# A fp32 encoder block on one core: weight tiles in pairs, and two tiles of a product in one VectorE instruction

## The chip, the cores and the metric

The kernel runs on one core of a Trainium2 chip. The metric is device time in microseconds (us), the median of the runs. A core has TensorE (PE, matmuls), VectorE (DVE), ScalarE (ACT), GpSimd (POOL) and SyncE (SP), each with a queue that it works off in order. They meet through semaphores. Here SP issues nearly all transfers, and POOL some that add to what lies in memory.

## The reference, cut to what matters

One layer over x of 256 rows and 1024 columns, all in fp32. The weight matrices make up nearly all of the traffic and of the matmuls:

```python
x = x + 0.5 * rmsnorm(swiglu(rmsnorm(x), w_in, w_down))        # FFN 1, d_ff 2816
h = rmsnorm(x); z = h @ w_in                                   # one wide projection
A = hgrn2(q, f, i, g)                                          # gated linear recurrence, chunks of 64
B = fox_attention(q, k, v, f)                                  # causal attention with forget gates
y = sigmoid(gate_A) * (A @ w_branch_a) + sigmoid(gate_B) * (B @ w_branch_b)
x = x + rmsnorm(y @ w_out)
x = x + rmsnorm(cross_attention(rmsnorm(x), rmsnorm(mem)))     # 4 heads, memory of 256 rows
x = x + 0.5 * rmsnorm(swiglu(rmsnorm(x), w_in, w_down))        # FFN 2
```

## The kernel before, in words

**Split operands.** Each fp32 operand is kept as a high part `hi` (a cast to fp32r on ACT) and a low part `lo` (source minus high part, a subtraction on DVE). A product is three matmuls: high by high, low by high, high by low (`MM`, L100). Activations and weights are both split, and the split of the weights is most of the work of DVE and ACT.

**Units.** The weights come as units of 128 x 1024 fp32 (512 KB). `load_split` loads one into a tile `raw` (SP), casts it (ACT, L153) and makes the low part (DVE, L155). `unit` does so on first use and keeps the tiles. Four memory tags matter: `raw` and `extra` with four tiles each, `hi` and `lo` with eight each. A tile is used again, in turn, once every reader of its last contents is done. `extra` also serves things that are not weights: some of the first loads (`head`), the recurrence's scratch (`early`, `qf`), the split keys `kp`, `brow`, `pT1`, `memT`, and the sums `ss`.

**Pairs of seven products.** In eight places (columns c = 4, 6, 9 of the first FFN and 3, 6, 9 of the second, one branch projection and the memory's value projection) two adjacent column blocks are computed by a scheme of seven products in place of eight. It needs sums of weight blocks. `sum_load` or `pair_load` fetches two tiles `sraw` from `extra`; POOL adds further blocks by transfers that accumulate (`more`, `pair_more`). `raws` fetches two plain blocks. `add` adds blocks on DVE, tile by tile (L596 in the FFNs, L1393 in the other two); `splits` casts and splits the two tiles one after the other (`split`, L173 and L174). Between the products PE does other work, in the FFNs mostly the down projection (`acc`).

**What sets the order.** A scheduler orders each engine's instructions by its own estimates and by priorities, under the constraints written in the code; each engine then runs its list in order. A change in the size of an instruction therefore changes the lists of all engines.

Of the kernel before, what the change touches and what calls it, by code (L numbers as in the profile page):

```python
# [18 lines left out]
P = 128  # L19
D = 1024  # L20
# [65 lines left out]
def block_kernel(ctx: ExitStack, tc: tile.TileContext, wts, head_in, gf_in, x_in, mem_in, memT_in, cols, rows, fbias, masks, out):  # L86
# [57 lines left out]
    def load_split(src, n=512, behind=None, parts=None):  # L144

        raw = wp.tile([P, D], F32, tag="raw", name=nm("raw"), bufs=4)
        hi, lo = parts or parts_of()
        r, h, l = raw, hi, lo
        if n < 512:
            r, h, l = (p.rearrange("p (k n) -> p k n", k=2)[:, :, :n] for p in (raw, hi, lo))  # L150
        loads.append(nc.sync.dma_start(r, src).ins)
        with tc.issue_after(behind[0]) if behind else nullcontext():
            casts.append(S.copy(h, r).ins)  # L153
        with tc.issue_after(behind[1]) if behind else nullcontext():
            los.append(V.tensor_tensor(out=l, in0=r, in1=h.bitcast(F32), op=ALU.subtract).ins)  # L155
        return hi, lo

    def unit(name, i):
        u = _AT[name] + i
        if u not in cache:  # L160
            cache[u] = load_split(wts[u - 4], behind=hold.get(u), parts=place.get(u))
        return cache[u]

    def chunk(name, c):
# [7 lines left out]
    def split(hi, lo, src):  # L172
        a = S.copy(hi, src)  # L173
        b = V.tensor_tensor(out=lo, in0=src, in1=hi.bitcast(F32), op=ALU.subtract)  # L174
        return a.ins, b.ins

    class Pair:

# [248 lines left out]
    def ffn(w_in, w_dn, X, r2, n_tok, i_row, first_half, second_half=None):  # L427
# [126 lines left out]
            return out, q, parts  # L554

        def sum_load(c, n, halves):
            t = []
            for j in range(2):
                r = wp.tile([P, D], F32, tag="extra", name=nm("sraw"), bufs=4)
                more(r, c, *halves[0], j, None)  # L560
                t.append(r)
            return t

        def more(r, c, k, n, j, op):
# [6 lines left out]
        def act_pair(c, between):  # L571
# [5 lines left out]
            def of_x(k):  # L577
                return lambda kk: (X.hi(4 * k + kk, 0, P), X.lo(4 * k + kk, 0, P))

            def splits(t):  # L580
                u = []
                for r in t:
                    p = parts_of()
                    split(p[0], p[1], r)
                    u.append(p)
                return u

            def raws(k, n):
                t = [wp.tile([P, D], F32, tag="raw", name=nm("raw"), bufs=4) for _ in range(2)]
                for j in range(2):  # L590
                    more(t[j], c, k, n, j, None)
                return t

            def add(t, o):
                for x, y in zip(t, o):
                    V.tensor_tensor(out=x, in0=x, in1=y, op=ALU.add)  # L596

            def product(ps, stat, u, start):
                for kk in range(4):
# [20 lines left out]
            add(sums, both)  # L620
            if c in FETCHED[w_in]:
                for j in range(2):
                    more(both[j], c, 1, 1, j, ALU.add)
            for _ in range(2 if c == 3 else 1):
                step_between()
            b4 = mm()
# [169 lines left out]

    X1 = Joined()
    xf1 = [m4([P, 4, T], n="xf") for _ in range(2)]  # L800
    heads, raw1 = [], []
    for kb in range(KB):
        heads.append(wp.tile([P, D], F32, tag="extra" if kb in (1, 2, 3, 4, 6) else "raw", name=nm("head"), bufs=4))
        n = HX if kb == 0 else 0
        if n:
            nc.scalar.dma_start(heads[kb][:, :n], head_in[kb, :, :n])
        loads.append(nc.sync.dma_start(heads[kb][:, n : HX + 512], head_in[kb, :, n:]).ins)
        if kb % 2 == 0:
            raw1.append(wp.tile([P, D], F32, tag="extra" if kb == 6 else "raw", name=nm("raw"), bufs=4))
# [10 lines left out]
    for kb in range(KB):  # L820
        if kb % 2 == 0:
            for c in range(2):
                cache[_AT["f1_in"] + 4 * c + kb // 2] = parts_of()
        for c in range(2):
            hi, lo = (p[:, kb % 2 * 512 : kb % 2 * 512 + 512] for p in cache[_AT["f1_in"] + 4 * c + kb // 2])
            w = heads[kb][:, HX : HX + 512] if c == 0 else raw1[kb // 2][:, kb % 2 * 512 : kb % 2 * 512 + 512]
            with tc.issue_after(lo_last):
                S.copy(hi, w)
# [29 lines left out]
    for i in range(2):  # L858
        place[_AT["i_a"] + i] = [wp.tile([P, D], F32R, tag="extra", name=nm("w"), bufs=4) for _ in range(2)]
    iv = [m4([P, 2, 512], n="iv") for _ in range(2)]  # L860
    for h in range(2):
        m = len(log)
# [77 lines left out]
    class Rec:  # L940


        def __init__(self, g):
            self.g, self.f = g, fT[g]
            self.aux = m4([P, D], n="aux")

            self.ATd = self.aux[:, 256:512]

            self.Es = wp.tile([P, D], F32, tag="extra", name=nm("early"), bufs=4)
            self.K, self.Q0 = kT_[g], qT_[g]  # L950
            self.Q = wp.tile([P, D], F32, tag="extra", name=nm("qf"), bufs=4).rearrange("p (b h t) -> p b h t", b=2, h=4)
# [131 lines left out]
    zf = [s1(8, name="zf") for _ in range(2)]  # L1083
    gf_last = {}
    for c in range(3):
        u = [load_split(gf_in[4 * c + i], GF) for i in range(4)]
        n = min(GF, D - c * GF)
        for h in range(2):
            ps = mm()
# [88 lines left out]

    kq = []
    for g in range(2):  # L1180
        kp = [wp.tile([P, D], F32R, tag="extra", name=nm("kp"), bufs=4).rearrange("p (i t) -> p i t", i=4) for _ in range(2)]
# [75 lines left out]

    def fox_pT(g, m):
        pT0 = m4([P, 4, T], n="pT0")
        pT1 = wp.tile([P, D], F32, tag="extra", name=nm("pT1"), bufs=4)[:, :512].rearrange("p (i s) -> p i s", i=4)  # L1260
        for h, b in ((0, 0), (1, 0), (1, 1)):
            tr = trp()
            with after(m + 5 * b):
# [43 lines left out]
    def gates(c):  # L1307
        u = chunk("gates", c)
        z = m4([P, 2, 512], n="zg")
        if c < 2:  # L1310
            brow = wp.tile([P, D], F32, tag="extra", name=nm("brow"), bufs=4)[:, :512]
# [57 lines left out]
        return wts[_AT[name] + 4 * (1 - n) + 2 * k + j - 4]  # L1369

    def pair_load(name, k, n, tag):
        t = []
        for j in range(2):
            r = wp.tile([P, D], F32, tag=tag, name=nm("sraw" if tag == "extra" else "raw"), bufs=4)
            loads.append(nc.sync.dma_start(r, pair_block(name, k, n, j)).ins)
            t.append(r)
        return t

    def pair_more(name, t, k, n):
        for j in range(2):  # L1380
            G.dma_start(t[j], pair_block(name, k, n, j), accum_op=ALU.add)

    def splits(t):
        u = []
        for r in t:
            p = parts_of()
            split(p[0], p[1], r)
            u.append(p)
        return u

    def add(t, o):
        for x, y in zip(t, o):
            V.tensor_tensor(out=x, in0=x, in1=y, op=ALU.add)  # L1393

    def product(ps, stat, u, start):
        for kk in range(4):
# [97 lines left out]
    next(pair)  # L1494
    summed(1, 1)

    memT_s = [wp.tile([P, 4, T], F32, tag="extra", name=nm("memT"), bufs=4) for _ in range(2)]
    for j in range(2):
        nc.sync.dma_start(memT_s[j], memT_in[:, 4 * j : 4 * j + 4, :])
    M = Joined()  # L1500
# [50 lines left out]
                half(X3, r3, c, G_MEM, m + (L_WO, L_MK)[c], m + (L_WO, L_MK)[c] + 16)  # L1551
    def mem_sums():
        a, b, d, e = (memT_s[k][:, :, h * P : h * P + P] for h in range(2) for k in range(2))
        ss = [wp.tile([P, 2, 4, P], F32, tag="extra", name=nm("ss"), bufs=4) for _ in range(2)]
# [140 lines left out]
    g3 = load_row(2)  # L1695
    for kb in range(4):
        hold[_AT["mo"] + kb] = marks[(1, 1, 3, 3)[kb]]
    for i in range(2):
        place[_AT["f2_in"] + i] = [wp.tile([P, D], F32R, tag="extra", name=nm("w"), bufs=4) for _ in range(2)]
    X4 = Joined()  # L1700
    r4 = [None, None]
    po = [[acc(), acc()], [acc(), acc()]]
# [110 lines left out]
```

## Time and profile before

| | |
|---|---|
| median of 3 runs | 767.61 us (767.55 to 768.75) |
| the profiled execution, first to last instruction | 765.6 us, mean granted clock 0.997 |
| around it, by the median | 2.0 us |
| PE busy | 756.7 us (99%) |
| DVE busy | 670.7 us (88%), 988 instructions |
| ACT busy | 520.6 us (68%), 841 instructions |
| read from memory | 152.91 MB, 201 GB/s over the span |

The page names lines and tiles: `lo<-sraw,hi` at L174 is a low part in a pair, `lo<-raw,hi` at L155 that of a unit. `DVE lo L155 <- ACT hi L153` says that DVE stood still until ACT had made that high part. In timelines the columns are start, duration, engine and line, with the idle time before it and its cause in brackets. x2 means two instructions in a row, whose time is given together.

### The profile page before, as it was taken

How to read it: one execution, taken by the hardware profiler on the slowest of the kernel's cores; microseconds unless marked ns; L12 is line 12 of the kernel's file. 1: busy time of each engine (PE TensorE's matmuls, PEld its weight loads, DVE VectorE, ACT ScalarE, POOL GpSimd, SP SyncE). 2: the span in 40 equal slices, each digit the busy share in tenths (PEclk: the TensorE clock that was granted, in tenths of full speed). 3: DMA queues.
4: the chain of work that ended last, by engine and by line, in shares of the span. 5: the costliest groups of instructions: out<-in, count | busy, mean ns of one | idle time of the engine just before them, and what ended most of it. 6: DMA issues, size and time to landing. Idle time of an engine off the chain costs nothing.

```text
span 765.6 us, 11740 instructions
## 1 busy us (share of the span) xinstructions
PE 756.7 (99%) x4302; PEld 642.1 (84%) x4302; DVE 670.7 (88%) x988; ACT 520.6 (68%) x841; POOL 27.2 (4%) x50
## 2 busy tenths in 40 slices
PE   9999999999999999999999999999999999999996
PEld 7888888888888998898888888888888888888885
DVE  6799998998678898888689888999989999998983
ACT  7677576688774669667567754875868567675662
POOL 0000000000000100200000000001000000000000
PEclk9999999999999999999999999999999999999998
DMA  9768677674655535835668965476386716558341
GB/s 344 238 257 247 212 240 275 170 261 174 223 169 149 185 122 185 290 135 163 210 220 226 267 202 184 160 284 130 124 283 202 251 66 232 208 191 288 125 140 55
DMA packets 46282, 154.73 MB, mean 202 GB/s; under 512 B 5289, under 2 KB 9009, under 8 KB 46225
## 3 DMA queue, kind: packets, MB, share of 16 engines
q1 hardware_dynamic: 43168, 144.83, 55.0%
q0 software_dynamic: 2624, 8.80, 6.4%
q8 instruction: 33, 0.54, 0.3%
q10 hardware_dynamic: 432, 0.37, 0.2%
q14 instruction: 25, 0.20, 0.1%
HBM read 152.91 MB, written 1.06 MB: 201 GB/s over the span
## 4 chain that ended last, share of the span: by engine, by line
PE 83%; DVE 9%; DMA 3%; ACT 2%; issue 2%; SPq 0%; POOL 0%; DVEq 0%; ACTq 0%; POOLq 0%
PE mm L100 44%; PE acc L100 30%; PE tr L100 5%; DVE lo L155 2%; DMA raw<-in_wts_dram 1%; PE tr L445 1%; DVE lo L174 1%; ACT hi L153 1%; DMA head<-in_head_dram 1%; DMA row<-rd 1%; PE tr L385 1%; DVE sraw L1393 1%; DVE xs L421 0%; DVE memT L1505 0%; DVE sx L174 0%
## 5 line engine op out<-in xcount | busy, mean ns | idle before, releaser
L155 DVE TENSOR_TENSOR lo<-raw,hi 128x1024 fp32r<-128x1024 f32 (+1 forms) x188 | 222.3, 1199 | 28.2 <-ACT hi L153 25.0
L153 ACT CAST hi<-raw 128x1024 fp32r<-128x1024 f32 (+1 forms) x188 | 190.5, 1032 | 48.5 <-DMA raw<-in_wts_dram 26.0
L100 PE MATMUL mm<-hi,hlT 128*128 128x512 f32 (+1 forms) x632 | 191.4, 381 | 0.0
L100 PEld LDWEIGHTS mm<-hi,hlT 128*128 128x128 f32 x632 | 116.8, 188 | 20.2
L100 PE MATMUL mm<-lo,hlT 128*128 128x512 f32 (+1 forms) x316 | 119.1, 381 | 0.0
L100 PE MATMUL acc<-hi,act 128*128 128x512 f32 x352 | 113.6, 390 | 0.0
L173 ACT CAST hi<-sraw 128x1024 fp32r<-128x1024 f32 x80 | 83.3, 1052 | 35.5 <-DVE sraw L596 17.5
L174 DVE TENSOR_TENSOR lo<-sraw,hi 128x1024 fp32r<-128x1024 f32 x80 | 96.0, 1220 | 1.7 <-ACT hi L173 1.4
L100 PE MATMUL mm<-hi,sx 128*128 128x512 f32 x280 | 90.7, 391 | 0.0
L100 PEld LDWEIGHTS acc<-hi,act 128*128 128x128 f32 x352 | 66.1, 188 | 13.4
L100 PE MATMUL acc<-lo,act 128*128 128x512 f32 x176 | 69.5, 395 | 0.0
L100 PEld LDWEIGHTS mm<-lo,hlT 128*128 128x128 f32 x316 | 59.3, 188 | 10.0
L100 PEld LDWEIGHTS mm<-hi,sx 128*128 128x128 f32 x280 | 52.5, 188 | 10.9
L100 PE MATMUL acc<-hlT,hi 128*128 128x512 f32 x240 | 60.9, 394 | 0.2 <-DVE hlT L373 0.2
L100 PE MATMUL mm<-lo,sx 128*128 128x512 f32 x140 | 54.9, 392 | 0.0
L100 PEld LDWEIGHTS acc<-hlT,hi 128*128 128x128 f32 x240 | 43.1, 189 | 8.2 <-DVE hlT L373 0.7
L174 DVE TENSOR_TENSOR lo<-raw,hi 128x1024 fp32r<-128x1024 f32 x32 | 38.3, 1220 | 2.4 <-ACT hi L173 2.3
L173 ACT CAST hi<-raw 128x1024 fp32r<-128x1024 f32 x32 | 33.0, 1052 | 9.1 <-DMA raw<-in_wts_dram 3.9
L100 PEld LDWEIGHTS acc<-lo,act 128*128 128x128 f32 x176 | 33.1, 188 | 6.4
L100 PE MATMUL acc<-lo,hT 128*128 128x512 f32 x96 | 37.8, 393 | 0.0
L100 PE MATMUL acc<-hi,hT 128*128 128x512 f32 x96 | 37.6, 392 | 0.1
L100 PE MATMUL acc<-hi,lT 128*128 128x512 f32 x96 | 37.3, 390 | 0.0
(329 smaller groups left out, 1232.1 us busy)
## 6 DMA issues: line engine op xcount, KB each, us to landing
raw<-in_wts_dram SPq DMA_DIRECT2D x215, 512.0 KB, 4.5
sraw<-in_wts_dram SPq DMA_DIRECT2D x32, 512.0 KB, 5.8
sraw<-in_wts_dram POOLq DMA_DIRECT2D x14, 512.0 KB, 5.9
raw<-in_gf_dram SPq DMA_DIRECT2D x12, 344.0 KB, 3.5
head<-in_head_dram SPq DMA_DIRECT2D x7, 392.0 KB, 6.4
grow<-in_rows_dram SPq DMA_DIRECT2D x4, 512.0 KB, 7.6
xs<-in_x_dram SPq DMA_DIRECT2D x2, 512.0 KB, 7.7
cb<-cd POOLq DMA_DIRECT2D x2, 512.0 KB, 5.3
```

What stands on the lines that cost most here:

```text
L100: log.append(PE.matmul(*args, **kw).ins)
L153: casts.append(S.copy(h, r).ins)
L155: los.append(V.tensor_tensor(out=l, in0=r, in1=h.bitcast(F32), op=ALU.subtract).ins)
L173: a = S.copy(hi, src)
L174: b = V.tensor_tensor(out=lo, in0=src, in1=hi.bitcast(F32), op=ALU.subtract)
L385: PE.transpose(blocks[-1][1], src(kb), ident)
L445: PE.transpose(trv[:, j, h * P : (h + 1) * P], ats[c, h][:, j * P : (j + 1) * P], ident)
L1393: V.tensor_tensor(out=x, in0=x, in1=y, op=ALU.add)
```

## The change: what it does

Every buffer of the four tags is a pair of tiles side by side, `[128, 2, 1024]`, with half as many of them, so that the memory is the same. A pair's tile is one object: it is used again when both halves are done. Within the pairs of seven products DVE makes the low parts of both halves by one subtraction of 128 x 2048 (L205), and adds both by one addition (L209). The casts stay one for each half (L204). Units are loaded two at a time; their casts (L177) and low parts (L172) stay one for each. What else used `extra` gets halves of a pair in turn (`extra`), and the first loads likewise halves of `raw` (`raw_half`).

```diff
+    def double(tag, name=None, dt=F32):
+        return wp.tile([P, 2, D], dt, tag=tag, name=nm(name or tag), bufs=4 if tag in ("hi", "lo") else 2)
+
     def parts_of():
-        return [wp.tile([P, D], F32R, tag=t, name=nm(t), bufs=8) for t in ("hi", "lo")]
...
+        return [double(t, dt=F32R) for t in ("hi", "lo")]
...
+    def extra(name, dt=F32):
+
+        if "extra" not in spare:
+            t = double("extra", name, F32)
+            spare["extra"] = t[:, 1]
+            r = t[:, 0]
+        else:
+            r = spare.pop("extra")
+        return r if dt is F32 else r.bitcast(dt)
...
+        for j in range(2):
+            loads.append(nc.sync.dma_start(r[:, j], srcs[j]).ins)
+            with tc.issue_after(behind[j][0]) if behind[j] else nullcontext():
+                casts.append(S.copy(h[:, j], r[:, j]).ins)
+            low(j, behind[j])
...
+    def splits(t):
+        p = parts_of()
+        for j in range(2):
+            S.copy(p[0][:, j], t[:, j])
+        V.tensor_tensor(out=p[1], in0=t, in1=p[0].bitcast(F32), op=ALU.subtract)
+        return halves_of(p)
+
+    def add(t, o):
+        V.tensor_tensor(out=t, in0=t, in1=o, op=ALU.add)
...
-            def splits(t):
-                u = []
-                for r in t:
-                    p = parts_of()
-                    split(p[0], p[1], r)
-                    u.append(p)
-                return u
...
-            def add(t, o):
-                for x, y in zip(t, o):
-                    V.tensor_tensor(out=x, in0=x, in1=y, op=ALU.add)
...
-            self.Es = wp.tile([P, D], F32, tag="extra", name=nm("early"), bufs=4)
+            self.Es = extra("early")
```

The first place is column 6 of the first FFN. On DVE before, from the adds of the two sums to the low parts of the third product (`sraw_944` and `sraw_946` are the sum's two tiles, `act` an activation's low part, `raw_1074` and `raw_1086` units of the down projection):

```order
L596 TENSOR_TENSOR sraw_944<-sraw_944,raw_1047 128x1024
L596 TENSOR_TENSOR sraw_946<-sraw_946,raw_1048 128x1024
L174 TENSOR_TENSOR act_628<-tr_978,act_628 128x512
L174 TENSOR_TENSOR lo_1054<-sraw_944,hi_1053 128x1024
L174 TENSOR_TENSOR lo_1058<-sraw_946,hi_1057 128x1024
L155 TENSOR_TENSOR lo_1076<-raw_1074,hi_1075 128x1024
L155 TENSOR_TENSOR lo_1088<-raw_1086,hi_1087 128x1024
```

On DVE now, from the add of the second product on (`lo_940` belongs to it, `lo_974` to the third, `lo_993` to the pair of units):

```order
L209 TENSOR_TENSOR sraw_878<-sraw_878,sraw_881 128x2048
L198 TENSOR_TENSOR act_597<-tr_907,act_597 128x512
L205 TENSOR_TENSOR lo_940<-sraw_878,hi_939 128x2048
L209 TENSOR_TENSOR sraw_878<-sraw_878,raw_969 128x2048
L205 TENSOR_TENSOR lo_974<-sraw_878,hi_973 128x2048
L172 TENSOR_TENSOR lo_993<-raw_991,hi_992 128x1024 x2
```

The add and the low part that needs it are now neighbours, and the act's low part has come ahead of `lo_940`. On ACT before, at the same place:

```order
L173 CAST hi_1014<-sraw_944 128x1024
L173 CAST hi_1018<-sraw_946 128x1024
L617 COPY vw_954<-mm_956 128x512
L173 CAST act_628<-tr_978 128x512
L173 CAST hi_1053<-sraw_944 128x1024
L173 CAST hi_1057<-sraw_946 128x1024
L153 CAST hi_1075<-raw_1074 128x1024
L153 CAST hi_1087<-raw_1086 128x1024
L173 CAST hi_1098<-raw_1047 128x1024
L630 COPY pc_955<-mm_1013 128x512
```

On ACT now (`vw` and `pc` are copies of a finished product out of PE's accumulators):

```order
L204 CAST hi_939<-sraw_878 128x1024
L637 COPY vw_886<-mm_888 128x512
L197 CAST act_597<-tr_907 128x512
L204 CAST hi_939<-sraw_878 128x1024
L204 CAST hi_973<-sraw_878 128x1024
L650 COPY pc_887<-mm_938 128x512
L204 CAST hi_973<-sraw_878 128x1024
L177 CAST hi_992<-raw_991 128x1024 x2
```

The second cast of `hi_939` stands behind a copy and a cast that wait for PE, and the second of `hi_973` behind the copy of the product before it.

The second place is the end of the memory's value projection, under the softmax. On ACT before (`pm` are the exponentials, `hi_5816` and `hi_5820` the sixth product's two tiles):

```order
L173 CAST hi_5816<-raw_5812 128x1024
L173 CAST hi_5820<-raw_5814 128x1024
L1649 ACT_TABLE_LOAD
L1649 ACTIVATE pm_5726,sm_5720<-acc_5693,mx_5719,sc_5691 128x256 x2
...
L298 ACT_TABLE_LOAD
L298 ACTIVATE warm_79<-ones 128x1
L173 CAST hT_5780<-cv_5782 128x512
L173 CAST hi_5836<-sraw_5580 128x1024
```

On ACT now (`hi_5449` is the sixth product's pair):

```order
L204 CAST hi_5449<-raw_5446 128x1024
L1664 ACT_TABLE_LOAD
...
L332 ACT_TABLE_LOAD
L332 ACTIVATE warm_79<-ones 128x1
L197 CAST hT_5417<-cv_5419 128x512
L1629 COPY pc_5241<-mm_5242 128x512
L204 CAST hi_5449<-raw_5446 128x1024
```

The second half's cast has moved from ahead of the eight exponentials to behind them.

The third place is column 3 of the second FFN, on DVE (`sx` are low parts of activation sums). Before:

```order
L596 TENSOR_TENSOR sraw_6528<-sraw_6528,raw_6653 128x1024
L174 TENSOR_TENSOR act_6410<-tr_6600,act_6410 128x512
L174 TENSOR_TENSOR sx_6525<-ss_6514,sx_6525 128x512
L596 TENSOR_TENSOR sraw_6530<-sraw_6530,raw_6654 128x1024
L174 TENSOR_TENSOR lo_6660<-sraw_6528,hi_6659 128x1024
L174 TENSOR_TENSOR lo_6664<-sraw_6530,hi_6663 128x1024
```

Now:

```order
L198 TENSOR_TENSOR act_6013<-tr_6188,act_6013 128x512
L198 TENSOR_TENSOR sx_6122<-ss_6111,sx_6122 128x512
L209 TENSOR_TENSOR sraw_6125<-sraw_6125,raw_6235 128x2048
L209 TENSOR_TENSOR sraw_6128<-sraw_6128,raw_6235 128x2048
L198 TENSOR_TENSOR sx_6244<-ss_6111,sx_6244 128x512
L205 TENSOR_TENSOR lo_6240<-sraw_6125,hi_6239 128x2048
```

The add now starts behind act and sx, and a second one, which had come earlier before, stands between it and the low part.

More of the change, by code (lines that the diff above doesn't have):

```diff
@@ L622, in act_pair @@
                 for j in range(2):
-                    more(both[j], c, 1, 1, j, ALU.add)
+                    more(both[:, j], c, 1, 1, j, ALU.add)
             for _ in range(2 if c == 3 else 1):
@@ L802, in block_kernel @@
     for kb in range(KB):
-        heads.append(wp.tile([P, D], F32, tag="extra" if kb in (1, 2, 3, 4, 6) else "raw", name=nm("head"), bufs=4))
+        heads.append(extra("head") if kb in (1, 2, 3, 4, 6) else raw_half("head"))
         n = HX if kb == 0 else 0
@@ L1371, in pair_load @@
     def pair_load(name, k, n, tag):
[L1372 removed]
+        t = double(tag, "sraw" if tag == "extra" else "raw")
         for j in range(2):
[L1374 to L1376 removed]
+            loads.append(nc.sync.dma_start(t[:, j], pair_block(name, k, n, j)).ins)
         return t
@@ L1380, in pair_more @@
         for j in range(2):
[L1381 to L1393, printed above, removed]
+            G.dma_start(t[:, j], pair_block(name, k, n, j), accum_op=ALU.add)
     def product(ps, stat, u, start):
@@ L1495, in block_kernel @@
     summed(1, 1)
-    memT_s = [wp.tile([P, 4, T], F32, tag="extra", name=nm("memT"), bufs=4) for _ in range(2)]
+    memT_s = [extra("memT").rearrange("p (k t) -> p k t", k=4) for _ in range(2)]
     for j in range(2):
@@ L1697, in block_kernel @@
         hold[_AT["mo"] + kb] = marks[(1, 1, 3, 3)[kb]]
-    for i in range(2):
-        place[_AT["f2_in"] + i] = [wp.tile([P, D], F32R, tag="extra", name=nm("w"), bufs=4) for _ in range(2)]
+    place[_AT["f2_in"]] = [double("extra", "w", F32R) for _ in range(2)]
     X4 = Joined()
```

63 lines of the change are left out of this document (35 added, 28 removed).

## The prediction

> **What bounds the kernel now.** I first read the page's busy times and the chain that ended last.
>
> ```profile
> PE 756.7 (99%) x4302; PEld 642.1 (84%) x4302; DVE 670.7 (88%) x988; ACT 520.6 (68%) x841; POOL 27.2 (4%) x50
> PE 83%; DVE 9%; DMA 3%; ACT 2%; issue 2%; SPq 0%; POOL 0%; DVEq 0%; ACTq 0%; POOLq 0%
> ```
>
> TensorE is busy for 756.7 of 765.6 us and carries 83% of the chain. A busy PE need not be PE at its peak, so next I asked what PE waited for (total us, times, longest), and how full the engines are in one early stretch (PE, PEld, DVE, ACT, POOL).
>
> ```profile
> PE tr L100 <- PEq L1802: 0.8, 1, 0.8
> PE acc L100 <- ACT hlT L372: 0.5, 1, 0.5
> PE acc L1662 <- DVE sm L1652: 0.3, 1, 0.3
> PE acc L100 <- ACT hi L828: 0.3, 1, 0.3
> PE acc L100 <- DVE hlT L373: 0.2, 1, 0.2
> 75.00:100.00 25.00, 25.00 (x116) 20.69 (x115) 24.92 (x28) 15.51 (x21) 1.69 (x2) 1.00 0.77 222
> ```
>
> These are all of PE's waits: 2.1 us. The granted clock is 1.00. So no more than 2.1 us can be won while the matmuls stay the same in number and size, which they do. But between 75 and 100 us VectorE is as full as PE, 24.92 of 25 us: what delays VectorE there soon delays PE. The kernel has little to win and much to lose.
>
> **The change, part by part: VectorE's own work.** The instructions that are merged, one by one, and a half-sized one for the slope:
>
> ```profile
> L174 DVE TENSOR_TENSOR lo<-sraw,hi 128x1024 fp32r<-128x1024 f32 x80 | 96.0, 1220 | 1.7 <-ACT hi L173 1.4
> L596 DVE TENSOR_TENSOR sraw<-sraw,raw 128x1024 f32<-128x1024 f32 x30 | 36.1, 1219 | 0.0
> L174 DVE TENSOR_TENSOR act<-tr,act 128x512 fp32r<-128x512 f32 x22 | 15.1, 686 | 1.7 <-ACT act L173 1.6
> ```
>
> 112 low parts become 56 and 50 adds become 25: 81 fewer. From 512 to 1024 columns the time grows by 1220 - 686 = 534 ns, so 2048 columns should take 1220 + 2 x 534 = 2288 ns. The trace has no such instruction. Its upper bound is two single ones, 2.44 us; I take the slope, 2.29. By durations a merge saves 0.15 us, but two back to back take 2.35 us together in the timeline below, so in a full queue it saves 0.06. Over 81 merges that is 5 to 12 us of VectorE time. PE waited for VectorE 0.5 us in all, so none of this is on PE's path by itself. The lower bound on its worth is zero.
>
> The Trainium skill ("Perfetto Trace Analysis", section "Optimizing Scalar/DVE Operations") puts a fixed cost of about 60 ns on each VectorE operation in SBUF and says that larger operations raise throughput where the engine is saturated. The back-to-back rows agree with the 60 ns. The same section says that where an engine is not saturated but makes bubbles on others, breaking instructions up lets work finish sooner. By the first rule the full window above should gain; by the second the change should lose. The rows below decide it.
>
> **What the merge does to the order of events.** The chain in a product is add, cast on ScalarE, low part. It overlapped tile by tile: the first tile was cast while the second was added. After the change no cast can start before the whole add has ended, and no low part before both casts have. The place to see it is the second pair of the first FFN (the ACT and DVE rows of the order are in the section on the change). Before, on DVE and then ACT:
>
> ```profile
> 96.94 2.36 DVE L596 TENSOR_TENSOR sraw<-sraw,raw 128x1024 f32<-128x1024 f32 x2
> 99.21 0.69 DVE L174 TENSOR_TENSOR act<-tr,act 128x512 fp32r<-128x512 f32 x1
> 99.81 2.35 DVE L174 TENSOR_TENSOR lo<-sraw,hi 128x1024 fp32r<-128x1024 f32 x2
> ...
> 96.18 0.59 ACT L617 COPY vw<-mm 128x512 f32<-128x512 f32 x1 [2.96 <-PE mm L100]
> 96.66 0.59 ACT L173 CAST act<-tr 128x512 fp32r<-128x512 f32 x1
> 98.19 2.18 ACT L173 CAST hi<-sraw 128x1024 fp32r<-128x1024 f32 x2 [0.94 <-DVE sraw L596]
> 104.43 0.58 ACT L630 COPY pc<-mm 128x512 f32<-128x512 f32 x1
> ```
>
> And what PE had there:
>
> ```profile
> 98.71 0.39 PE L100 MATMUL mm<-hi,sx 128*128 128x512 f32 x1
> ...
> 104.15 0.39 PE L100 MATMUL mm<-hi,sx 128*128 128x512 f32 x1
> ```
>
> The isolated chain now takes 2.29 + 2.1 (two casts) + 2.29 = 6.7 us, where four singles, each starting 2.35 - 1.22 = 1.13 after the last, took 4.6: the second tile is 2.1 us later, the first 3.2. VectorE is idle for 2.1 us of it wherever nothing else stands between add and low part, which is so in most pairs.
>
> At this place it is worse, because both casts are needed at once. The second cast of the earlier product (hi_939) now stands on ACT behind the copy vw and the cast of act, which wait for PE: it runs from 97.2 to 98.2, and the merged low part from 98.2 to 100.5. PE, with one high matmul and eight of the down projection ahead of its first low one, arrives at 98.71 + 9 x 0.227 = 100.75 (twelve take 2.72 us in the chain's rows below): covered by a hair. Then the next add runs 100.5 to 102.8, the first cast to 103.9, the copy pc to 104.4, the second cast to 105.4, and the cast hi_992, which the down projection needs, to 106.4; the low part to 107.8. PE ends its product at 103.25, does four matmuls (104.15) and one more (104.4), and then stands until 106.45 for hi_992, does four (107.35) and stands until 107.8. That is 2.05 + 0.45 = **2.5 us**.
>
> The first pair has the same chain without such a queue:
>
> ```profile
> 60.33 2.35 DVE L596 TENSOR_TENSOR sraw<-sraw,raw 128x1024 f32<-128x1024 f32 x2
> ...
> 67.96 2.75 PE mm L100 x12
> 70.71 2.72 PE acc L100 x12
> ```
>
> The merged low part would end at 60.33 + 6.7 = 67.0, 1.2 us ahead of PE's first low matmul (68.2). The product before it has a merged add, too, and may bring up to 1.5 us of lag with it: **0.4**.
>
> **The memory value product.** It ends under the softmax, where ScalarE is full:
>
> ```profile
> 536.80 1.05 ACT L173 CAST hi<-raw 128x1024 fp32r<-128x1024 f32 x1 [3.07 <-issue]
> 543.87 1.28 ACT L298 ACT_TABLE_LOAD   x1
> 545.27 0.60 ACT L173 CAST hT<-cv 128x512 fp32r<-128x512 f32 x1
> 547.21 0.58 ACT L1614 COPY pc<-mm 128x512 f32<-128x512 f32 x1
> ...
> 539.61 1.22 DVE L174 TENSOR_TENSOR lo<-raw,hi 128x1024 fp32r<-128x1024 f32 x1
> 544.89 1.23 DVE L1653 TENSOR_TENSOR pm<-pm,sm 128x1024 f32<-128x1024 f32 x1
> ...
> 546.28 0.40 PE L100 MATMUL tr<-lo,hlT 128*128 128x512 f32 x1
> ```
>
> Before, both casts of the sixth product were done at 537.9, ahead of the softmax. In the changed order the second one stands behind all exponentials, the second table load and the copy pc. With the table loaded at 545.15, hT to 545.9, pc to 546.3 and the cast to 547.3, the merged low part, which now serves the first half as well, ends at 549.7. PE wants it at 546.28: 3.4 us. The exponentials may start up to 1 us sooner, since VectorE has 1.22 us less ahead of the maxima; the least is 1.1, what the last product alone loses by waiting for both casts. I take the rows with a little off: **3.0**.
>
> **The second FFN.** Where it enters its pairs:
>
> ```profile
> 626.16 1.22 DVE L596 TENSOR_TENSOR sraw<-sraw,raw 128x1024 f32<-128x1024 f32 x1
> 628.90 1.23 DVE L174 TENSOR_TENSOR lo<-sraw,hi 128x1024 fp32r<-128x1024 f32 x1 [0.39 <-ACT hi L173]
> 629.86 0.39 PE L100 MATMUL mm<-hi,sx 128*128 128x512 f32 x1
> ```
>
> In the new order two whole adds follow on 626.16 (to 630.7), a small sx (631.35) and the low part (to 633.65). PE now has one matmul, twelve of the down projection and one more ahead: 629.86 + 14 x 0.227 = 633.0. **0.7**, rounded up for the semaphores.
>
> **Buffers in pairs.** The memory is the same, but a slot is free only when both halves are. Loads wait in SP's queue for low parts already, and ACT for loads:
>
> ```profile
> SPq L151 <- DVE lo L155: 311.1, 126, 13.3
> ACT hi L153 <- DMA raw<-in_wts_dram: 26.0, 27, 3.5
> ```
>
> The first load of a pair comes one low part (1.13 us) later. The rows above show a cover of some 3 us (a low part done at 101.0 for a matmul at 104.4), which hides it. At the start, two of the eight heads' transfers wait for a pair instead of a tile. One recurrence's two scratch tiles are now a pair, so the first kp can only be cast after that recurrence's products; that is hidden, since kp is read late:
>
> ```profile
> L100 PE MATMUL acc<-kp,qp x24: 278/283/363, 336.6 to 340.9; 128*128 128x256 f32 x24
> ```
>
> All these, the third pair of each FFN and the branch pair together: **0.8**, an estimate between 0 and 3.
>
> **The sum.** 0.4 + 2.5 + 3.0 + 0.7 + 0.8 = 7.4 us. The span goes from 765.6 to 773.0; with the 2.0 us that lie between it and the median, 767.6 becomes 775.0.
>
> **Rivals.**
> - *VectorE's relief wins (faster).* VectorE is full in the window above, and 5 to 12 us of it are freed. The Trainium skill's rule on grouping, above, makes this the outcome. Against it: PE waits only 2.1 us, of which 0.8 is its own start. At best 767.6 - 1.3 to 2.1, so 765.5 to 766.3.
> - *All of it is hidden.* The low parts of the early pair stood 3.4 us ahead of PE (101.0 for 104.4), and PE's order was laid out anew around the later ones. For it: the first low part at 100.75 is just met. Against: 107.8 and 549.7 are not. 766.1 to 769.1.
> - *Nothing is hidden.* Each of the eight pairs loses its 2.1 us, since VectorE is too full to catch up: 8 x 2.1 = 17, so 784.4. Against: VectorE is idle for 12% of the span, in which a lag is made good, and the first pair's chain above ends 1.2 us early.
> - *The pairs of raw decide.* A load held up by 1.13 us reaches ACT late in those 27 waits. If a quarter of them find no cover, 7 x 1.13 = 8 us come on top: 783. Against: the 4 slots' worth of memory is unchanged.
>
> **How the numbers follow.** Forecast (768.5 to 781): 0.65. Relief: 0.07. Hidden: 0.10. Nothing hidden: 0.10. Raw pairs: 0.08. The range 767.5 to 783 leaves out the relief, a part of the hidden case and the upper half of the last two, about 0.2. Within 0.2% (1.5 us, what a measurement here can tell) lies most of the hidden case: 0.09. Faster 0.08, slower 0.83.
>
> **What would show it.** In the trace of the changed kernel: merged instructions of about 2.29 us, 56 and 25; PE's waits up from 2.1 to about 9 us, on lo and hi of the pairs, the largest near 105 us and 546 to 550 us; VectorE idle by about 2 us between an add and its low part; busy VectorE 5 to 12 us lower, PE's matmuls unchanged. I am wrong if PE's waits stay under 3 us, or if they lie on units (raw) rather than on pairs.

## The result, and the profile after

| | before | after |
|---|---|---|
| median of 4 runs | 768.18 us (767.55 to 769.38) | 791.76 us (789.45 to 793.24) |
| ratio | 1 | 1.0313 [1.0293, 1.0334] |
| profiled execution, first to last instruction | 765.6 us | 787.6 us |
| mean granted clock | 0.997 | 0.991 |

The kernel became 3.1% slower. The direction was predicted; the loss is three times the predicted 7.4 us and lies above the range. The page after, its busy times and the shares of the chain that ended last:

```profile
PE 766.2 (97%) x4302; PEld 644.9 (82%) x4302; DVE 665.3 (84%) x907; ACT 517.9 (66%) x841; POOL 25.8 (3%) x50
PE 74%; DVE 13%; DMA 5%; ACT 4%; issue 3%; SPq 0%; POOL 0%; DVEq 0%; ACTq 0%; POOLq 0%
L205 DVE TENSOR_TENSOR lo<-sraw,hi 128x2048 fp32r<-128x2048 f32 x40 | 91.5, 2289 | 20.5 <-ACT hi L204 20.3
```

VectorE did what was asked of it: 81 instructions fewer, 2289 ns each for the merged ones, 670.7 - 665.3 = 5.4 us less busy. But it now stands 20.3 us ahead of low parts of sums, waiting for casts. Before, it was 3.7 us in all pairs:

```profile
DVE lo L174 <- ACT hi L173: 3.7, 7, 1.3
```

PE's share of the chain fell from 83% to 74%. All of PE's waits after (total us, times, longest), but for the 0.8 us at its start, which it has before as well:

```profile
PE acc L100 <- DVE lo L172: 4.2, 2, 4.0
PE mm L100 <- DVE lo L205: 3.0, 3, 2.5
PE acc L100 <- ACT hi L177: 2.7, 2, 1.8
PE mm L100 <- ACT hi L204: 2.0, 1, 2.0
PE acc L1677 <- DVE pm L1668: 1.0, 1, 1.0
PE mm L100 <- ACT vw L658: 0.9, 1, 0.9
```

With the 0.8 they sum to 14.6 us, 12.5 more than before. Just under half of it, 4.2 + 2.7, is put down to units (L172, L177), which the change leaves single: what waits in VectorE's and ScalarE's queues behind the pairs is late too. The larger stops in PE's timeline, the idle time in brackets (the rest are of 0.2 to 0.3 us):

```profile
106.52 1.24 PE L100 MATMUL acc<-hi,act 128*128 128x512 f32 x4 [1.84 <-ACT hi L177]
154.87 0.50 PE L100 MATMUL mm<-hi,sx 128*128 128x512 f32 x1 [0.94 <-ACT vw L658]
176.64 0.96 PE L100 MATMUL acc<-hi,act 128*128 128x512 f32 x3 [0.82 <-ACT hi L177]
434.69 0.50 PE L100 MATMUL mm<-lo,fs 128*128 128x512 f32 x1 [2.48 <-DVE lo L205]
472.56 0.65 PE L100 MATMUL acc<-lo,hT 128*128 128x512 f32 x1 [3.97 <-DVE lo L172]
563.29 1.06 PE L1677 MATMUL acc<-ident,pm 128*128 128x128 f32 x8 [0.97 <-DVE pm L1668]
566.33 0.49 PE L100 MATMUL mm<-hi,sx 128*128 128x512 f32 x1 [1.97 <-ACT hi L204]
```

After three of them PE also ran at half clock. Windows after (window, length, PE, PEld, DVE, ACT, POOL, clock, DMA, GB/s):

```profile
107.53:110.94 3.41, 3.27 (x8) 2.46 (x8) 3.41 (x4) 3.41 (x4) 0.00 (x0) 0.50 0.02 5
435.21:438.62 3.41, 3.41 (x9) 2.68 (x9) 1.80 (x1) 0.00 (x0) 1.44 (x2) 0.50 0.68 105
472.75:476.17 3.42, 3.42 (x9) 2.54 (x9) 3.16 (x3) 0.00 (x0) 0.00 (x0) 0.50 0.42 131
```

Each episode is 3.41 us at a clock of 0.50, so it costs half of that: 1.7 us each, 5.1 in all. Before, the clock shows 1.00 up to PE's end:

```profile
0.00:761.00 761.00, 756.68 (x4302) 642.12 (x4302) 669.02 (x984) 520.65 (x841) 27.23 (x50) 1.00 0.62 203
```

Of the 22.0 us by which the span grew, stops are 12.5 and the slow clock 5.1. The remaining 4.4 us are in matmuls whose records are longer or further apart near the stops (the first after a stop shows 0.50 us for 0.39); I did not trace them to rows. By place: with the matmuls numbered in order in both traces, after lags behind before by nothing at 99 us of before, by 4.2 us at 112, 7.2 at 199, 7.4 at 418, 18.2 at 473, 17.2 at 544, 20.8 at 561 and 22.0 at the end. So the second pair of the first FFN brings 4.2 us, the third 3.0, the branch and what follows it 10.9, and the memory's value product 3.6.

### The profile page after: what moved, and what is told of

It is laid out like the page before. It is cut to its first block, busy times and chain, and to the rows that moved or that the text cites. A ratio compares the mean times of both kernels' runs of the same rounds, so it can differ in the third digit from the quotient of the medians.

```text
span 787.6 us, 11454 instructions
## 1 busy us (share of the span) xinstructions
PE 766.2 (97%) x4302; PEld 644.9 (82%) x4302; DVE 665.3 (84%) x907; ACT 517.9 (66%) x841; POOL 25.8 (3%) x50
## 4 chain that ended last, share of the span: by engine, by line
PE 74%; DVE 13%; DMA 5%; ACT 4%; issue 3%; SPq 0%; POOL 0%; DVEq 0%; ACTq 0%; POOLq 0%
PE mm L100 35%; PE acc L100 32%; PE tr L100 5%; DMA raw<-in_wts_dram 4%; DVE lo L205 3%; DVE lo L172 3%; DVE sraw L209 2%; ACT hi L204 2%; PE tr L419 1%; PE tr L479 1%; ACT pm L1664 1%; DMA head<-in_head_dram 0%; DMA row<-rd 0%; DVE zg L1423 0%; ACT hi L177 0%
## 5 line engine op out<-in xcount | busy, mean ns | idle before, releaser
L172 DVE TENSOR_TENSOR lo<-raw,hi 128x1024 fp32r<-128x1024 f32 (+1 forms) x188 | 222.1, 1198 | 32.2 <-ACT hi L177 30.0
L177 ACT CAST hi<-raw 128x1024 fp32r<-128x1024 f32 (+1 forms) x188 | 190.0, 1032 | 50.8 <-DMA raw<-in_wts_dram 39.7
L204 ACT CAST hi<-sraw 128x1024 fp32r<-128x1024 f32 x80 | 81.4, 1050 | 44.9 <-DVE sraw L209 33.5
L205 DVE TENSOR_TENSOR lo<-sraw,hi 128x2048 fp32r<-128x2048 f32 x40 | 91.5, 2289 | 20.5 <-ACT hi L204 20.3
L209 DVE TENSOR_TENSOR sraw<-sraw,raw 128x2048 f32<-128x2048 f32 x17 | 38.7, 2289 | 3.9 <-DMA raw<-in_wts_dram 3.7
L204 ACT CAST hi<-raw 128x1024 fp32r<-128x1024 f32 x32 | 32.6, 1050 | 12.0 <-DMA raw<-in_wts_dram 8.7
```

Of the source, the lines that this page charges most:

```text
L172: los.append(V.tensor_tensor(out=l[:, js], in0=r[:, js], in1=h[:, js].bitcast(F32), op=ALU.subtract).ins)
L177: casts.append(S.copy(h[:, j], r[:, j]).ins)
L204: S.copy(p[0][:, j], t[:, j])
L205: V.tensor_tensor(out=p[1], in0=t, in1=p[0].bitcast(F32), op=ALU.subtract)
L209: V.tensor_tensor(out=t, in0=t, in1=o, op=ALU.add)
```

## The experiments

The questions were which part of the change costs: the buffers in pairs, the merged adds or the merged low parts; and, for the low parts, whether it is the length of the instruction, the wait for both casts, a place too late in the program (theory C where a text uses letters), or the order of what stands in the engines' queues (theory E). Ratios are against the kernel before, run on the same chip alongside.

**Buffers in pairs alone** (pairs_only):

```diff
 def splits(t): ...
-        V.tensor_tensor(out=p[1], in0=t, in1=p[0].bitcast(F32), op=ALU.subtract)
+            V.tensor_tensor(out=p[1][:, j], in0=t[:, j], in1=p[0][:, j].bitcast(F32), op=ALU.subtract)
 def add(t, o):
-        V.tensor_tensor(out=t, in0=t, in1=o, op=ALU.add)
+        for j in range(2):
+            V.tensor_tensor(out=t[:, j], in0=t[:, j], in1=o[:, j], op=ALU.add)
```

> The changed kernel with its buffers in pairs, but every add and every low part of a pair again as two instructions of 128x1024. Theory A, the pairs of buffers cost the time (a load waits until both halves of the pair before it are split): the long stops of the branch products (2.5 us near 434 and 4.0 us near 472 us in the changed kernel, 10 us of delay with the slow clock behind them) stay, and the time is 778 to 784 us. Theory B, the merged instructions cost it (no cast before the whole add, no low part before both casts): those stops go with the ones near 105 and 566 us, and the time is 767 to 770 us. If both share it, 775 to 782, with the stops near 105 and 566 gone and those near 434 and 472 still there.

769.93 us, 1.0037 [1.0025, 1.0048]. VectorE's waits in its pairs:

```profile
DVE lo L205 <- ACT hi L204: 5.7, 5, 3.3
```

The buffers alone cost about 3 us (0.0037 x 767). Nearly all of the loss comes with the merging.

**Low parts merged, adds single** (lo_merged: only `add` as in pairs_only):

> Pairs of buffers and merged low parts; the adds are again two instructions. Theory A (buffers): 788 to 793, about as the changed kernel. Theory B (merged chain): the casts start one add (1.1 us) earlier, so a good third of what the merges cost is back, 780 to 787.

793.12 us, 1.0335 [1.0300, 1.0369]: all of the loss. The third that was to come back with single adds (780 to 787) did not. VectorE waits 28.7 us for casts in its pairs (`DVE lo L205 <- ACT hi L204`, 19 times).

**Adds merged, low parts single** (add_merged: only `splits` as in pairs_only):

> Pairs of buffers and merged adds; the low parts are again two instructions. Theory A (buffers): 788 to 793. Theory B (merged chain): the first low part no longer waits for the second cast, which in the changed kernel stood behind copies out of PE near 105 us and behind the softmax near 566 us; most of the merges' cost is back, 770 to 780.

772.78 us, 1.0077 [1.0052, 1.0101], so 0.0040 or 3 us above pairs_only. On top of merged low parts the merged adds bring nothing that these runs can tell (1.0313 against 1.0335, intervals that overlap). The low parts are the cause. VectorE's wait in its pairs is 15.8 us here, not far from the 20.3 after, at a quarter of the loss: how long VectorE stands in all does not tell the cost, only which of these waits reach PE.

**Another form of the buffers** (ring_raw_hl): `raw`, `hi` and `lo` are one long tile each, of which pairs are cut, so that a reader waits for what it reads and not for a whole pair. Some products in it seem to read a tile that a later unit has already replaced; its time is read with that in mind.

```diff
+        if tag not in ring:
+            ring[tag] = [wp.tile([P, 2 * n, D], F32R if tag in ("hi", "lo") else F32, tag=tag, name=nm(tag), bufs=1), 0]
+        i = ring[tag][1] % n
+        ring[tag][1] += 1
+        return ring[tag][0][:, 2 * i : 2 * i + 2]
```

> The changed kernel with merged adds and low parts, but the tiles of raw, hi and lo lie in one long tile for each tag, cut into pairs, so that each half is free for its next load or cast as soon as its own readers are done; extra stays in pairs. Theory A (release by pairs): the stops near 434 and 472 us go or shrink to under 1 us, the time falls by 8 to 12 us to 780 to 784. Theory B (merged instructions): 788 to 793, those stops stay.

795.16 us, 1.0385 [1.0342, 1.0428]. It has a stop of 9.7 us at its start that the others do not have, so the total says little. Inconclusive, but one place is told: at the branch product a stop of 2.1 us is still there though no reader waits for a whole pair, so it does not come from the buffers' form.

```profile
442.15 0.50 PE L100 MATMUL mm<-lo,fs 128*128 128x512 f32 x1 [2.13 <-DVE lo L214]
```

**Length or the wait for both casts** (cross): single adds, and two low parts per pair as before, of the same size as before, but each cut across both tiles, so that each needs both casts.

```diff
-        V.tensor_tensor(out=p[1], in0=t, in1=p[0].bitcast(F32), op=ALU.subtract)
+        for k in range(0, D, 512):
+            V.tensor_tensor(out=p[1][:, :, k : k + 512], in0=t[:, :, k : k + 512], in1=p[0][:, :, k : k + 512].bitcast(F32), op=ALU.subtract)
```

> Single adds and two low parts for each pair, each of 128 x (2 x 512): the first takes the left half of both tiles, the second the right half. So each is as long as a single one (1.2 us) but waits for both casts. Theory C (waiting for both casts costs the time): 785 to 793, as with the merged low part. Theory D (the length of the merged instruction, 2.29 us without a first result at half time, or the order that the scheduler makes of so long an instruction): 768 to 775, as with single ones. A value between says how much is each.

804.16 us, 1.0477 [1.0448, 1.0507]: worse than the merge. Of cross, the group of VectorE's low parts of sums, and then PE's waits:

```profile
L206 DVE TENSOR_TENSOR lo<-sraw,hi 128x1024 fp32r<-128x1024 f32 x80 | 95.4, 1219 | 26.2 <-ACT hi L204 26.0
```

```profile
PE mm L100 <- DVE lo L206: 8.2, 11, 3.2
PE tr L100 <- DVE lo L206: 6.0, 3, 4.1
```

The instructions take 1219 ns as before, 988 of them on VectorE as before, and the loss is larger, above the 785 to 793 of theory C too. No long instruction is needed for the loss; that was theory D. It does not price the length by itself: PE asks for the second of the two low parts after three matmuls (3 x 0.227 = 0.7 us), while it follows the first by 1.13 us. That cross is 11 us slower than lo_merged is in part the clock: seven windows of 3.41 us at half clock in its trace, three in that of lo_merged, so 4 x 1.7 = 6.8 us of the 15.4 between the two profiled spans.

**One cast for both tiles** (one_cast): after, with `S.copy(p[0], t)` for the two casts, so that nothing can stand between them in ScalarE's queue.

> The changed kernel (merged adds and low parts), but the two casts of a pair are one instruction of 128 x 2048 on ScalarE, so that no copy or softmax can stand between them. Theory C1 (a second cast stuck in ScalarE's queue behind work that waits for PE is what delays the low parts): 772 to 780, and the stops near 105 and 566 us go. Theory C2 (the chain add, casts, low part is too long wherever it lies): 788 to 796.

785.28 us, 1.0239 [1.0196, 1.0282], between the two forecasts. About 6 us of the loss went (0.0074 x 767; by the two intervals 1 to 11), the rest stayed. The second cast stuck behind other work in ScalarE's queue is a part of the cause, not most of it: VectorE still waits 31.4 us for casts in its pairs (`DVE lo L204 <- ACT hi L203`, 22 times, in an execution that was slower than the median).

**Priority** (prio): the pairs' casts and low parts inside `with tc.high_priority():`.

> The changed kernel with the pairs' casts and low parts at high priority in the scheduler. Theory C1 (order in the queues): the second casts come ahead of the copies and the time falls to 772 to 782. Theory C2 (length of the chain): within 4 us of the changed kernel, 786 to 796; high priority may also push back evacuations that PE waits for.

792.02 us, 1.0328 [1.0307, 1.0349]. No change against after.

**Only the plain blocks** (lo_blocks): single adds, and of 56 low parts only the 16 of plain blocks (`splits(raw)`) merged.

```diff
-            product(b4, of("baed"), splits(raw), False)
+            product(b4, of("baed"), splits(raw, True), False)
```

> Single adds; only the 16 low parts of plain blocks (fetched for a product of their own, no add ahead of them) are merged, the other 40 stay two instructions. Theory C (both casts, after a chain with an add) sees little here, since their source has no add ahead: 769 to 774. If merged low parts cost in proportion to their number, 16 of 56 of some 20 us: 774 to 778.

776.91 us, 1.0130 [1.0109, 1.0150]: 7 us above pairs_only, a third of the 21 for 16 of 56 low parts, so about in proportion, and not the little that theory C gave a source without an add. By difference the sums, 40 of 56, bring the other two thirds; no run merged them alone. In lo_blocks the memory value product has its stop as in after, 1.98 us before 552.43.

**Earlier in the program** (ahead: every add and split written one product sooner; ahead_ffn: in the FFNs alone). If the split came merely too late, this should bring it back.

```diff
+            u1 = splits(sums)
             add(sums, both)
...
-            product(b1, of_x(0), splits(sums), True)
+                u = splits(sums)
+            product(b1, of_x(0), u1, True)
```

> The changed kernel (merged adds, merged low parts, pairs), with the adds and splits of each of the seven products written one product earlier in the program, so that the scheduler may place them a product (some 5 us) further ahead of PE; the work is the same. Theory C (the low part that waits for both casts comes 2 to 3 us too late, and nothing else is wrong): most of the stops go, 770 to 778. Theory E (the wait delays VectorE's and ScalarE's whole queues, units and evacuations too, or the four pairs of hi and lo leave no room to be further ahead): 785 to 795.

794.77 us, 1.0348 [1.0318, 1.0378].

> The same only in the six pairs of the two FFNs; the branch and memory products are as in the changed kernel. Of the changed kernel's 22 us over before, 7 lie in the first FFN up to 176 us and 1 in the second. Theory C: 782 to 786, those 8 us gone, the stops near 434, 472 and 566 us as they were. Theory E: 788 to 795.

798.54 us, 1.0394 [1.0370, 1.0417]. Neither helps; the second is worse than after, and slower than either theory had it. In ahead_ffn the stops in the first FFN have moved, and the largest there is again at a unit's cast:

```profile
168.84 1.97 PE L100 MATMUL acc<-hi,act 128*128 128x512 f32 x4 [2.19 <-ACT hi L177]
```

That an earlier pair takes room in the queue from the units behind it would explain this; it is not shown. Nor did the splits run a whole product sooner. In ahead, at the second pair, the third product's casts stand behind the copy of a product that PE has yet to finish, and the low part starts at 107.76. In after it started at 105.56, with PE 3.2 us less behind, so it came only some 1 us sooner:

```profile
105.25 0.59 ACT L654 COPY pc<-mm 128x512 f32<-128x512 f32 x1 [4.82 <-PE mm L100]
```

So writing the split sooner does not help; what a split that does run a product sooner would bring, these two runs do not show.

**VectorE with room** (light_single, light_merged): the units get no low parts, PE reads the high part in their place; this leaves out that part of the computation. light_single is pairs_only with it, light_merged is after with it.

```diff
-        parts = parts or parts_of()
+        parts = parts or [double("hi", dt=F32R)]
+        parts = [parts[0]] * 2
...
-            low(j, behind[j])
+            los.append(casts[-1])
```

> A control: the buffers in pairs and single adds and low parts in the products, but no low parts for the units of load_split (188 of VectorE's instructions, some 222 us of its 670, are left out; PE reads the high part in their place, so the number of matmuls is the same). VectorE is then under 60% busy and raw frees sooner. Both theories: PE sets the pace, 764 to 769 us.

> The same with merged adds and merged low parts as in the changed kernel, and no low parts for the units. Theory E (VectorE is full, so that each wait for a second cast delays all that stands behind it, and the lag is not made good): with a VectorE that has time, the cost nearly goes: within 4 us of light_single. Theory C (the merged low part itself comes too late for PE, whatever else VectorE has to do): 10 us or more over light_single, with stops near 105 and 566 us.

VectorE is busy 466.9 us in light_single (61%) and 462.0 us in light_merged (60%). light_single: 767.56 us, 0.9998 [0.9986, 1.0011]. light_merged: 777.54 us, 1.0123 [1.0102, 1.0143]. The merge costs 10 us here, against some 21 (0.0313 - 0.0037) with the units' low parts: the number that theory C gave, not the 4 us at most of theory E. In light_merged no matmul of the FFNs' pairs stops; PE has two large stops, and the rows of ScalarE and VectorE ahead of them are:

```profile
448.85 0.79 PE L100 MATMUL tr<-lo,hT 128*128 128x512 f32 x1 [3.87 <-DVE lo L206]
554.44 0.63 PE L100 MATMUL mm<-hi,sx 128*128 128x512 f32 x1 [2.57 <-ACT hi L205]
442.88 1.05 ACT L205 CAST hi<-raw 128x1024 fp32r<-128x1024 f32 x1 [1.57 <-DMA raw<-in_wts_dram]
445.26 1.04 ACT L205 CAST hi<-raw 128x1024 fp32r<-128x1024 f32 x1
446.51 2.28 DVE L206 TENSOR_TENSOR lo<-raw,hi 128x2048 fp32r<-128x2048 f32 x1
```

So about half of the loss needs a full VectorE and goes when it has room. The other half lies at the ends of the branch and the memory product: the two stops, 6.4 us, and an episode at half clock behind each, 2 x 1.7, are the whole 9.8 us between the spans of the two runs. At the branch the first cast waits for a late load and the second comes 2.4 us after it (442.88 and 445.26). A single low part could have started at 443.9; the merged one starts at 446.5. PE came to it at 444.98, so a single one, done at 445.2, would have held PE for some 0.2 us (an estimate from these rows) in place of 3.87. In light_single ScalarE has the same casts in the same order there, the first half's low part starts at 439.63, 1.1 us after the start of its cast, and PE does not stop. At the memory product the second cast stands behind the softmax (at 551.43, the first at 542.65), as it does after.

Every variant gets its own lists from the scheduler, and no run holds the lists fixed while the low parts are merged. The evidence that the wait for both casts makes the stops, and not a new order, is these two places, where ScalarE's order is nearly the same with and without the merge (the memory product in pairs_only follows below). For the FFNs it is argued from them.

## Why the prediction was right in direction and wrong in size

**Durations and VectorE's own work: right.** Forecast 2.29 us and 5 to 12 us of relief, measured 2289 ns and 5.4 us. As forecast, none of the relief showed in the time.

**The second pair of the first FFN (2.5 us): right in place and nearly in size.** The forecast had PE stand until 106.45 for the cast `hi_992`; it stood until 106.52 for it. On VectorE and ScalarE after:

```profile
100.72 2.29 DVE L209 TENSOR_TENSOR sraw<-sraw,raw 128x2048 f32<-128x2048 f32 x1
105.56 2.29 DVE L205 TENSOR_TENSOR lo<-sraw,hi 128x2048 fp32r<-128x2048 f32 x1 [2.54 <-ACT hi L204]
103.05 1.05 ACT L204 CAST hi<-sraw 128x1024 fp32r<-128x1024 f32 x1 [4.68 <-DVE sraw L209]
104.48 1.05 ACT L204 CAST hi<-sraw 128x1024 fp32r<-128x1024 f32 x1
105.42 2.00 ACT L177 CAST hi<-raw 128x1024 fp32r<-128x1024 f32 x2
```

Add, cast, cast, low part in a row, each waiting for the whole of the last, as the order had shown. The stop is 1.84 us. What was not forecast is the 1.7 us of slow clock behind it. Of the 0.45 us after it, for the low part, 0.15 shows: the four matmuls end at 107.76, the low part at 107.85 (forecast 107.8), and PE's matmul on it starts at 107.91.

**The memory value product (3.0 us): right.** The stops at 563.29 and 566.33, and one of 0.3 behind them, make 3.3. The cast that had been done ahead of the softmax before comes behind it now, and the low part behind the cast:

```profile
563.28 1.05 ACT L204 CAST hi<-raw 128x1024 fp32r<-128x1024 f32 x1
564.36 2.29 DVE L205 TENSOR_TENSOR lo<-raw,hi 128x2048 fp32r<-128x2048 f32 x1
```

By the profile the two stops are put down to other work, the softmax's `pm` and the first cast of the seventh product (which ends at 566.28). But the low part ends at 566.65, and PE's matmul on it starts at 566.71: without them PE could not have been further. The order of the casts alone costs nothing. In pairs_only the second cast stands behind the softmax too, but the first half's low part waits for its own cast alone and runs ahead of the softmax, and the longest stop of PE there is 0.3 us:

```profile
538.27 1.21 DVE L205 TENSOR_TENSOR lo<-raw,hi 128x1024 fp32r<-128x1024 f32 x1
545.17 1.05 ACT L204 CAST hi<-raw 128x1024 fp32r<-128x1024 f32 x1
```

So it was not the merge that moved the second cast behind the softmax, as the forecast took it, but it is the merge that makes PE pay for it.

**The first pair (0.4) and the second FFN (0.7): small, as forecast.** One stop of 0.2 us in the first pair (at 73.6 us, on `lo`, L205), and no stop of PE in the second FFN.

**The step that failed most: 0.8 us for "all these, the third pair of each FFN and the branch pair together".** I worked out four of the eight pairs by rows and put the other four into one small term, with the cover of one good place for all. Measured, the branch and what follows it have stops of 2.48 and 3.97 us and two slow-clock episodes, 9.9 us; the third pair of the first FFN has stops of 0.94, 0.82 and 0.2, 2 us. That is 12 us where 0.8 stood. At the branch, before:

```profile
406.29 1.46 SPq L1375 DMA_DIRECT2D raw<-in_wts_dram  x2
417.61 2.35 DVE L1393 TENSOR_TENSOR sraw<-sraw,raw 128x1024 f32<-128x1024 f32 x2
419.95 2.37 DVE L174 TENSOR_TENSOR lo<-sraw,hi 128x1024 fp32r<-128x1024 f32 x2
```

and after:

```profile
417.50 0.88 SPq L1402 DMA_DIRECT2D raw<-in_wts_dram  x2
427.99 2.29 DVE L209 TENSOR_TENSOR sraw<-sraw,raw 128x2048 f32<-128x2048 f32 x1 [2.71 <-DMA raw<-in_wts_dram]
430.31 2.00 ACT L204 CAST hi<-sraw 128x1024 fp32r<-128x1024 f32 x2 [4.42 <-DVE sraw L209]
432.35 2.29 DVE L205 TENSOR_TENSOR lo<-sraw,hi 128x2048 fp32r<-128x2048 f32 x1 [1.46 <-ACT hi L204]
```

Before, the first low part starts 419.95 - 417.61 = 2.3 us after the first add, without a wait. After, it is 4.4 us, and VectorE waits 2.7 us for the load besides. The load was issued 11.2 us later than before, when the whole had lost 7.4 (the matmul that starts at 406.31 before starts 7.4 us later after). SP waited for units' low parts before it could issue it, in both kernels (before from 395 to 410 us, then after from 400 to 420):

```profile
SPq L1375 <- DVE lo L155: 14.4, 2, 13.6
```

```profile
SPq L1402 <- DVE lo L172: 10.2, 1, 10.2
```

Late low parts make late loads: that is a loop that the term of 0.8 left out. But it does not cost by itself. pairs_only, where PE lags 0.6 us here, issues the load at 409.25, so 2.4 of the 3.8 us beyond the lag come with the pairs of buffers, and there is no stop. Over the whole kernel ScalarE waits for units' loads for 26.0 us before, 37.0 in pairs_only and 39.7 after. In pairs_only:

```profile
417.83 2.35 DVE L210 TENSOR_TENSOR sraw<-sraw,raw 128x1024 f32<-128x1024 f32 x2
420.38 2.36 DVE L205 TENSOR_TENSOR lo<-sraw,hi 128x1024 fp32r<-128x1024 f32 x2 [0.20 <-ACT hi L204]
```

The load's second half lands at 418.8 in pairs_only and at 427.9 after, 9.1 us later, of which PE's lag is 6.8. From that landing to the end of the low parts pass 4.0 us in pairs_only (the first add starts before the second half is there) and 6.7 after, where add, casts and low part each wait for the whole. So of the 5.1 us by which the low parts come later against PE than in pairs_only, 2.8 are the merged chain and the rest is the later landing; what made the landing later stays open.

The stop of 3.97 us at 472.56 has two halves, of which the order showed neither as risky: ScalarE's casts waited for loads (1.8 us at 460, on `raw`), and VectorE, which itself waited 1.8 us for a row from memory, had the units' low parts behind 6.5 us of other work, so that four of them ran back to back only when PE was already standing. After:

```profile
464.75 0.49 DVE L1520 SCALAR_TENSOR_TENSOR memT<-memT,cols_s,row 128x256 f32<-128x256 f32 x1 [1.81 <-DMA row<-rd]
471.27 4.63 DVE L172 TENSOR_TENSOR lo<-raw,hi 128x1024 fp32r<-128x1024 f32 x4
```

That this stop comes with the merge is shown by its absence in pairs_only; which of its links is the decisive one stays open.

**The slow clock (5.1 us): no term.** The rows of before could not show it, since PE never stopped there for more than 0.8 us.

**Buffers in pairs: about 3 us measured (pairs_only), at the top of my 0 to 3.** I had called the late release hidden, so the cover was too hopeful here as well. With the merged low parts the chain costs 21 more.

**The rivals.** Relief and "all hidden" fell. "Nothing is hidden" (784.4) was nearest in time, but not in kind: the second FFN hid its three pairs, while others lost several times their 2.1 us. "The pairs of raw decide" was wrong about the buffers, yet right that PE would wait for units: 6.9 of 14.6 us. What I had held to be a sign against my theory was its second half.

## What to carry to other kernels

An instruction that is merged over two tiles starts when the later of its inputs is there; everything behind it in the engine's queue waits too (units' low parts stood behind the wait of 2.54 us at 105.56), and a saving of 5.4 us of busy time turned into 24 us of time. Before merging, walk each place through the queues: how long between the first and the second input, what stands between them, and who waits behind, the transfers that these free included. Where the places that were walked show a loss, the ones that were not are no rounding term.

## What the runs showed of the hardware that was not expected

A stop of PE of some 2 us can be followed by 3.41 us at half clock, which costs another 1.7 us: nearly as much as the stop. Whether it does is not told by the length of the stop. In one execution the shorter stop can be the one that loses the clock: in one_cast 1.62 us did, the stop before 175.80, and 1.99 us did not:

```profile
484.74 0.50 PE L100 MATMUL acc<-lo,hT 128*128 128x512 f32 x1 [1.99 <-DVE lo L172]
```

It is told by where the stop falls. In all fourteen traces the clock changes only at the edges of a grid of 3.413 us: in after the three half-clock windows above start 327.68 and 37.54 us apart, 96 and 11 times 3.413. Cut along the grid, one_cast shows the two stops, each with the window behind it:

```profile
173.70:177.12 3.42, 1.73 (x7) 0.78 (x6) 1.34 (x2) 2.10 (x2) 0.00 (x0) 1.00 0.79 271
177.12:180.53 3.41, 3.41 (x8) 2.76 (x9) 2.31 (x2) 1.04 (x1) 0.00 (x0) 0.50 0.52 155
480.90:484.32 3.42, 1.85 (x9) 1.20 (x7) 3.42 (x8) 1.60 (x5) 0.00 (x0) 1.00 0.00 0
484.32:487.73 3.41, 2.99 (x13) 2.50 (x14) 3.41 (x5) 0.00 (x0) 0.00 (x0) 1.00 0.58 193
```

The stop of 1.62 us lies whole in one window, and the next is at half clock. That of 1.99 us is cut by an edge into 1.57 and 0.42, and the clock stays. Counted over the fourteen traces (PE's idle times of over 0.06 us): each of the 21 windows in which PE stood for 1.85 us or more is followed by half clock, none of those with less than 1.5 us is, and of the 18 between, 9 are. So what a stop costs is in part luck: it depends on how it lies to the grid, and the grid lies differently in each trace (its first edge is 0.2 us behind the first instruction in before, 1.7 in after, 3.0 in one_cast).

The Trainium skill ("TensorE: Matmul & The Clock Gate", section "Part 1: The HAM clock gate (the "warmup" mystery)") describes a clock of two states, half and full, set by activity in a window of about 3.4 us that runs on its own, with the half state after at least one idle window. The two states, the 3.4 us and the grid agree with these rows. By its rule of a whole idle window none of the three stops of after should have lost the clock: even that of 3.97 us fills only 3.22 of a window's 3.41 us. The windows counted above show that somewhat more than half a window is enough.
